# Key pages, key rows and value rows moved in one transfer each, in a hybrid conformer and stick-breaking attention step on one core

## The chip, the core and the metric

The kernel runs on one core of a Trainium2 chip. A core has five engines that run side by side, each through its own instructions in order: TensorE (PE, matmuls into PSUM; PEld is its weight load), VectorE (DVE), ScalarE (ACT), GpSimd (POOL) and SyncE (SP, which here only issues DMA transfers). 16 DMA engines move data between the device's DRAM and SBUF, the on-chip memory of 128 partitions. Engines wait for each other and for transfers by semaphores. The metric is device microseconds of one execution, lower is better.

## The reference

One inference step of a trunk of two layers, for a prompt of 512 new tokens and for 8 sequences that each add 4 tokens to 256 cached ones (their keys and values lie in pages of 128 tokens). Layer 0 mixes tokens by a conformer convolution, layer 1 by stick-breaking attention; each is followed by a gated convolutional FFN. All data is fp32. Cut to the layer that the change touches:

```python
D_MODEL, SEQ, DEC_BATCH, DEC_SEQ, PAST_LEN, PAGE_SIZE, N_HEADS, HEAD_DIM = 1024, 512, 8, 4, 256, 128, 16, 64

def stick_breaking_block(q, k, v, bias, q_start):
    z = einsum('bqhd,bkhd->bhqk', q, k) * HEAD_DIM ** -0.5 + bias[None, :, None, None]
    valid = k_pos[None, :] < q_pos[:, None]
    log_fail = where(valid, log_sigmoid(-z), 0.0)
    after = cumsum(log_fail, axis=3, reverse=True) - log_fail
    weights = where(valid, exp(log_sigmoid(z) + after), 0.0)
    return einsum('bhqk,bkhd->bqhd', weights, v)

# in run_trunk, layer 1
qkv = (h @ attn_w_qkv).reshape(b, t, 3, N_HEADS, HEAD_DIM)
q, k, v = qkv[:, :, 0], qkv[:, :, 1], qkv[:, :, 2]
k_all, v_all = concatenate([k_past, k], 1), concatenate([v_past, v], 1)   # k_past: pages of cache_k by page_table
x = x + stick_breaking_attention(q, k_all, v_all, bias, past_len).reshape(b, t, -1) @ attn_w_o
# k and v of the new tokens are outputs too, as rows (token, head, head_dim)
```

## The kernel before

Activations are kept transposed: `xT`, `qT` and `kT` hold 128 of the 1024 model columns on the partitions, in 8 column blocks `c`, and tokens along the free dimension. A projection takes a block of 256 weight columns of 1 MB (`raw`, loaded by SP, two buffers), splits it on ScalarE and VectorE into a high and a low part (`whi`, `wlo`) and multiplies both by the high and low parts of the activations (`XH`, `XL`), which is the L2163 to L2165 matmuls in the attention layer.

The attention stage works on column blocks `c` (two heads each). For each it projects keys (`keys`) and values (`values`) of the prompt in two halves `h` of 256 and 288 tokens (the second half also has the 32 new tokens of the 8 sequences), then computes logits, scans and products of the pair of heads (`pair`). Beside that the stage works on the cached pages of the 8 sequences:

- `key_page` loads one page of keys, 128 tokens by 1024 numbers, into one of three buffers of `xT`'s memory (`page_t`; the layer's input was saved to DRAM before and is read back at the end, `xsave`). 16 heads lie in four groups of four, `x`; the partition is 32 times the group plus a token number. VectorE then turns blocks of 32 by 32 (L2283), so that the head dimension comes onto the partitions, and a group of matmuls into `dz` (L2301) makes the logits of one pair of sequences from four pages. There are 16 pages and so four dz groups; pages 0 to 2 are asked for before the attention stage, right after `xsave`.
- `keys` copies the projected keys to `kT`, turns them in blocks of 32 by 32 on VectorE (`kr`, two buffers, L2207) and stores them as rows of the output `k_p`, with four transfers for each half (L2212).
- `values` copies the projected values to SBUF on ScalarE (`vT`, L2221), transposes them by two matmuls with the identity (`to_rows`, PSUM tile `one`, L2193) and copies the rows to `vtok` on VectorE (L2225); there they serve the products with the attention weights (`av`, L2494) and are stored to `v_p` (L2228).
- Pages of values are gathered by POOL (L2050) after the pages of keys, into the same three buffers.

The order of the instructions is written by a planner, `Plan`: every operation is entered with its engine, an estimated cost in us and what it reads and writes; `Plan.run` then plays the list through and issues the operations in the order in which they come free, by a priority. The times of `Plan` are estimates only and set the order of instructions on each engine; on the chip each engine follows its own list and waits where it must. For SP, `Plan` counts a fixed 0.7 us until the next issue, and the operation's cost until its data has landed. All of SP's transfers stand in one queue.

Of the kernel before, what the change touches and what calls it, by code (L numbers as in the profile page):

```python
# [9 lines left out]
F32 = mybir.dt.float32  # L10
# [7 lines left out]
P = 128  # L18
# [87 lines left out]
class Plan:  # L106
# [5 lines left out]
    def __init__(self, eager=EAGER, chain=0.0, shifts=""):  # L112
        self.eager = eager
        self.shifts = shifts

        self.chain = chain
        self.ops = []
        self.writes, self.adds, self.reads = {}, {}, {}
        self.rings = {}
        self.follows = {}  # L120
        self.lift, self.urgent = {}, {}
        self.forms, self.change = {}, 0.0
        self.fill = set()

    def op(self, eng, cost, fn, r=(), w=(), a=(), follows=None, lift=0.0, urgent=0.0, after=(), form=None):

        i = len(self.ops)
        deps = set(after)
        for x in r:
            deps |= self.writes.get(x, set()) | self.adds.get(x, set())  # L130
        for x in a:
            if self.reads.get(x):
                self.writes[x] = self.writes.get(x, set()) | self.reads[x] | self.adds.get(x, set())
                self.reads[x], self.adds[x] = set(), set()
            deps |= self.writes.get(x, set())
        for x in w:
            deps |= self.writes.get(x, set()) | self.reads.get(x, set()) | self.adds.get(x, set())
        for x in r:
            self.reads.setdefault(x, set()).add(i)
        for x in a:  # L140
            self.adds.setdefault(x, set()).add(i)
        for x in w:
            self.writes[x], self.reads[x], self.adds[x] = {i}, set(), set()
        for x in (*r, *w, *a):
            b = x[0] if isinstance(x, tuple) else x
            if isinstance(b, Plan.Buf):
                if not b.users and b.before is not None:
                    b.after |= {b.before.users[0]}
                if not b.users and b.old is not None:
                    b.after |= set(b.old.users)  # L150
                deps |= b.after
                b.users.append(i)
        deps.discard(i)
        self.ops.append((eng, cost, fn, deps))
        if lift:
            self.lift[i] = lift
        if urgent:
            self.urgent[i] = urgent
        if follows is not None:
            self.follows[i] = follows  # L160
        if form is not None:
            self.forms[i] = form
        return i

    class Buf:
# [26 lines left out]
    def run(self):  # L192
# [24 lines left out]
        while any(ready.values()):  # L217
# [21 lines left out]
            if eng == "pe":  # L239
                form = self.forms.get(i)  # L240
            last[eng] = i
            free[eng] = t + (cost if eng != "sp" else 0.7)
            for u in users[i]:
                left[u] -= 1
                start[u] = max(start[u], t + cost + self.lag(eng, self.ops[u][0]))
# [5 lines left out]
def tile_trunk(  # L251
# [219 lines left out]
    def uid(s):  # L471
        _n[0] += 1
        return f"{s}_{_n[0]}"
# [1566 lines left out]

    def key_page(t, j):

        pages = cache_k[0, bass.ds(numbers[j], 1)].rearrange("o (q p) (x h) d -> o x p q (h d)", p=32, x=4)
        for x in range(4):
            nc.sync.dma_start(out=t[32 * x:32 * x + 32, :].rearrange("p (q r) -> p q r", q=4), in_=pages[0, x])

    cv = cache_v.rearrange("o n p h d -> (o n p) (h d)")

# [92 lines left out]
    def acost(n):  # L2141
        return 0.1 + n * 0.95e-3
# [41 lines left out]
            prepare(slot + SPLIT_BUFS)  # L2184
        return pt

    def to_rows(src, r):

        rows = psum("one")

        def turn():
            for b in range(2):
                pe.transpose(rows()[:, b * P:(b + 1) * P], src(b), ident)  # L2193

        plan.op("pe", 0.22, turn, r=r, w=[rows])
        return rows, (lambda: rows()[:, :2 * P].rearrange("p (b d) -> p b d", b=2))

    def keys(c, h):
        c0, n = (SA, SB)[h]
        pt = project(k0 + TURNS.index(("k", c)), h)  # L2200
        plan.op("act", acost(256), lambda: act.copy(kT[:, c, c0:c0 + 256], pt()[:, :256]),
                r=[pt], w=[("k", c, h)] + ([("ktp", i) for i in range(4)] if c >= 4 else []))
        if h:
            plan.op("act", 0.2, lambda: act.copy(kT_s[:, c, :], pt()[:, 256:n]), r=[pt], w=[("kT_s", c)])
            plan.op("pool", 1.2, lambda: place_k(c), r=[("kT_s", c)], w=[("kn", c)])
        kr = sbuf("kr", 2 * P, 2)
        plan.op("dve", 0.15 + 256 * 1.1e-3, lambda: dve.transpose(kr(), kT[:, c, c0:c0 + 256]), r=[("k", c, h)], w=[kr])  # L2207

        def store():
            for a in range(4):  # L2210
                rows = slice(32 * a, 32 * a + 32)
                nc.sync.dma_start(out=k_p[0, 0, c0:c0 + 256].rearrange("(b i) h d -> i b (h d)", i=32)[:, :, c * P + 32 * a:c * P + 32 * a + 32],  # L2212
                                  in_=kr()[rows].rearrange("i (b j) -> i b j", j=32))

        plan.op("sp", 7.0, store, r=[kr])

    def values(c, h):
        n = (SA, SB)[h][1]
        pt = project(k0 + TURNS.index(("v", c)), h)
        vt = plan.tile("vT", 2, lambda: vts_.tile([P, SA[1]], F32, tag="vT", name=uid("vT"), bufs=2))  # L2220
        plan.op("act", acost(256), lambda: act.copy(vt(), pt()[:, :256]), r=[pt], w=[vt])  # L2221
        if h:
            plan.op("act", 0.2, lambda: act.copy(vT_s[:, c, :], pt()[:, 256:n]), r=[pt], w=[("vT_s", c)])
        rows, src = to_rows(lambda b: vt()[:, b * P:(b + 1) * P], [vt])
        plan.op("dve", 0.38, lambda: dve.tensor_copy(vtok[c % 3][:, 2 * h:2 * h + 2, :], src()),  # L2225
            r=[rows], w=[("vtok", c % 3, h)])
        if h:
            plan.op("sp", 3.0, lambda: nc.sync.dma_start(out=vpv[:, :, c * P:(c + 1) * P], in_=vtok[c % 3]),  # L2228
                    r=[("vtok", c % 3, 0), ("vtok", c % 3, 1)])

    def new_rows(src, r, dst):

# [12 lines left out]

        plan.op("pe", 0.5, turn, r=r, w=[rows], form="r64")
        plan.op("act", 0.35, lambda: act.copy(new_s, rows()[:, :2 * P]), r=[rows], w=["new", "Qz"])
        plan.op("sp", 3.0, store, r=["new"])


    def page(i):

        t = plan.tile("page", PAGE_BUFS, lambda: page_t[i % PAGE_BUFS])
        if i < PAGE_BUFS:
            plan.op("held", 0.0, lambda: None, w=[t])
            return t
        if i < 2 * NB:
            plan.op("sp", 2.0, lambda: key_page(t(), i), w=[t, ("asked", i)])
        else:
            plan.op("pool", 1.05, lambda: gather(t(), i % (2 * NB), cv), w=[t, ("asked", i)])  # L2260
        plan.op(f"page{i}", 6.0 if i < 2 * NB else 4.0, lambda: None, r=[("asked", i)], w=[(t, 1)])
        return t
# [7 lines left out]
    def page_logits(m):  # L2270
# [17 lines left out]
        def logits():  # L2288
            for odd in range(2):
# [5 lines left out]
                    parts = [(0, KW, kt)]  # L2295
                for e in range(2):
                    for lo, n, src in parts:
                        keys_of = src.rearrange("p (q k j) -> p k q j", k=NC, j=32)
                        for u in range(4):
                            k = 4 * (u % 2) + 2 * (u // 2) + e  # L2300
                            pe.matmul(z()[32 * u:32 * u + 32, (m % 2) * KW + lo:(m % 2) * KW + lo + n],  # L2301
# [322 lines left out]
```

## Time and profile before

| what | value |
|---|---|
| runs | 1256.1, 1256.89, 1257.56 us (median 1256.89) |
| profiled execution | 1256.83 us, of which the span from its first to its last instruction 1255.1 us |
| granted TensorE clock | 0.998 |
| attention stage | from about 585 us (`xsave`) to 831 us (`xT` read back) |
| DMA, whole span | 139661 packets, 142.40 MB, mean 113 GB/s |
| DMA packets under 512 B | 24045 |

The page gives busy times of the engines; a TensorE that is busy all the time is not one at its peak. The share of DMA is the mean over 16 engines. Views of a stretch (from A to B us) give the same sums for that stretch alone: in the DMA row of a stretch each digit is the busy share, in tenths, of a fortieth of it, and the row below it counts packets, and how many of them were under 512 B. In the chain of waits each piece is what the next one waited for.

### The profile page before, as it was taken

The numbers are of one execution on the slowest core, as the hardware profiler recorded it, in microseconds if no ns is written. First come the engines' busy times: TensorE is split into PE (matmuls) and PEld (weight loads), VectorE is DVE, ScalarE is ACT, GpSimd is POOL, SyncE is SP. The second block draws the span as 40 slices with busy tenths as digits, with TensorE's granted clock in tenths as the row PEclk, the third lists the DMA queues.
The fourth block names the chain that finished last, engine by engine and source line by source line (L and its number), as shares of the span: only waits on it lengthen the run. The fifth ranks groups of instructions, "written<-read, shape, count | busy, mean of one in ns | idle before, by whom it ended". The sixth has DMA issues, their size and how long they took to land.

```text
span 1255.1 us, 26652 instructions
## 1 busy us (share of the span) xinstructions
PE 1239.3 (99%) x10742; PEld 1187.2 (95%) x10742; DVE 1011.2 (81%) x1700; ACT 709.8 (57%) x1421; POOL 173.8 (14%) x363
## 2 busy tenths in 40 slices
PE   9999999999999999999999999999999999999997
PEld 8997699999999999999988888999999999999997
DVE  7999887988987886878969897646979987887863
ACT  7793584646655454445545887744636645455453
POOL 5000014111001000000242344000101001000000
PEclk9999999999999999999999999999999999999999
DMA  7455423123233233244379465232123232233121
GB/s 223 129 168 152 129 68 117 35 86 114 80 112 118 68 106 99 92 145 161 97 190 246 128 173 159 71 126 85 49 88 102 93 120 93 80 108 118 60 79 72
DMA packets 139661, 142.40 MB, mean 113 GB/s; under 512 B 24045, under 2 KB 132773, under 8 KB 139266
## 3 DMA queue, kind: packets, MB, share of 16 engines
q1 hardware_dynamic: 133134, 120.29, 32.1%
q0 software_dynamic: 6400, 20.41, 5.2%
q8 instruction: 84, 1.38, 0.5%
q14 instruction: 39, 0.32, 0.1%
q10 hardware_dynamic: 4, 0.01, 0.0%
HBM read 129.34 MB, written 12.18 MB: 113 GB/s over the span
## 4 chain that ended last, share of the span: by engine, by line
PE 81%; DVE 14%; DMA 2%; ACT 2%; issue 1%; SPq 0%; POOL 0%; DVEq 0%; ACTq 0%
PE acc L1635 5%; PE acc L1634 5%; PE acc L1633 5%; PE acc L759 4%; PE acc L760 4%; PE acc L761 4%; PE av L896 3%; DVE wlo L401 3%; PE av L1412 3%; PE av L1413 3%; PE av L1414 3%; PE tr L1413 3%; PE tr L1412 3%; PE tr L1414 3%; PE tr L1633 3%; PE tr L1635 3%
## 5 line engine op out<-in xcount | busy, mean ns | idle before, releaser
L398 ACT CAST whi<-raw 128x1024 fp32r<-128x1024 f32 (+2 forms) x247 | 224.7, 913 | 123.5 <-PE av L1413 24.8
L401 DVE TENSOR_TENSOR wlo<-raw,whi 128x1024 fp32r<-128x1024 f32 (+2 forms) x247 | 258.7, 1050 | 33.0 <-ACT whi L398 31.5
L759 PE MATMUL acc<-XH,whi 128*128 128x288 f32 (+1 forms) x384 | 112.7, 294 | 0.0
L761 PE MATMUL acc<-XH,wlo 128*128 128x288 f32 (+1 forms) x384 | 110.3, 287 | 0.9 <-DVE wlo L401 0.9
L760 PE MATMUL acc<-XL,whi 128*128 128x288 f32 (+1 forms) x384 | 110.3, 287 | 0.0
L1412 PE MATMUL av<-HH,whi 128*128 128x288 f32 (+1 forms) x280 | 83.2, 297 | 0.5 <-DVE xT L1735 0.5
L1413 PE MATMUL av<-HL,whi 128*128 128x288 f32 (+1 forms) x280 | 82.6, 295 | 0.0
L1635 PE MATMUL acc<-TH,wlo 128*128 128x272 f32 x288 | 82.6, 287 | 0.0
L1634 PE MATMUL acc<-TL,whi 128*128 128x272 f32 x288 | 82.6, 287 | 0.0
L1633 PE MATMUL acc<-TH,whi 128*128 128x272 f32 x288 | 82.5, 287 | 0.0
L1414 PE MATMUL av<-HH,wlo 128*128 128x288 f32 (+1 forms) x280 | 82.2, 293 | 0.0
L1682 ACT COPY G<-acc 128x272 f32<-128x272 f32 (+1 forms) x72 | 26.8, 372 | 93.8 <-PE acc L1635 93.8
L2163 PE MATMUL acc<-XH,whi 128*128 128x256 f32 (+1 forms) x264 | 79.7, 302 | 0.0
L1412 PE MATMUL tr<-HH,whi 128*128 128x256 f32 (+1 forms) x280 | 78.5, 280 | 0.0
L1413 PE MATMUL tr<-HL,whi 128*128 128x256 f32 (+1 forms) x280 | 78.4, 280 | 0.0
L1414 PE MATMUL tr<-HH,wlo 128*128 128x256 f32 (+1 forms) x280 | 78.3, 280 | 0.0
L2165 PE MATMUL acc<-XH,wlo 128*128 128x256 f32 (+1 forms) x264 | 75.7, 287 | 0.0
L2164 PE MATMUL acc<-XL,whi 128*128 128x256 f32 (+1 forms) x264 | 75.7, 287 | 0.0
L759 PEld LDWEIGHTS acc<-XH,whi 128*128 128x128 f32 x384 | 72.2, 188 | 1.4 <-issue 0.4
L761 PEld LDWEIGHTS acc<-XH,wlo 128*128 128x128 f32 x384 | 72.1, 188 | 1.1 <-DVE wlo L401 1.1
L760 PEld LDWEIGHTS acc<-XL,whi 128*128 128x128 f32 x384 | 72.2, 188 | 0.3
L1573 DVE SCALAR_TENSOR_TENSOR cv<-G,fprm,cv 128x560 f32<-128x560 f32 x88 | 69.5, 797 | 0.5
(464 smaller groups left out, 4343.0 us busy)
## 6 DMA issues: line engine op xcount, KB each, us to landing
raw<-in_ffn_w_gate_dram SPq DMA_DIRECT2D x22, 1024.0 KB
raw<-in_ffn_w_up_dram SPq DMA_DIRECT2D x22, 1024.0 KB
raw<-in_ffn_w_down_dram SPq DMA_DIRECT2D x24, 768.0 KB
raw<-in_attn_w_qkv_dram SPq DMA_DIRECT2D x12, 1024.0 KB
xT<-in_cache_k_dram SPq DMA_DIRECT2D x64, 128.0 KB
raw<-in_conv_w_in_dram POOLq DMA_DIRECT2D x6, 1024.0 KB, 6.8
rep<-glu SPq DMA_DIRECT2D x36, 142.0 KB
raw<-in_conv_w_out_dram POOLq DMA_DIRECT2D x4, 1024.0 KB, 6.4
```

The costliest lines, as they stand in the source:

```text
L398: act.copy(hi[:, k, :], src[:, k])
L401: dve.tensor_tensor(lo[:, k, :], src[:, k], hi[:, k, :], op=ALU.subtract)
L759: pe.matmul(o, hi[:, k, :], XH[:, k, c0:c0 + n], start=(k == 0), stop=False)
L760: pe.matmul(o, hi[:, k, :], XL[:, k, c0:c0 + n], start=False, stop=False)
L761: pe.matmul(o, lo[:, k, :], XH[:, k, c0:c0 + n], start=False, stop=(k == NC - 1))
L1412: pe.matmul(o, hi[:, j + k, :], xh, start=(start and k == 0), stop=False, **kw)
L1413: pe.matmul(o, hi[:, j + k, :], xl, start=False, stop=False, **kw)
L1414: pe.matmul(o, lo[:, j + k, :], xh, start=False, stop=(stop and k == len(xs) - 1), **kw)
L1633: pe.matmul(o, hi[:, j + k, :], xh, start=(start and k == 0), stop=False, **kw)
L1634: pe.matmul(o, hi[:, j + k, :], xl, start=False, stop=False, **kw)
L1635: pe.matmul(o, lo[:, j + k, :], xh, start=False, stop=(k == 3), **kw)
L2163: pe.matmul(o, hi[:, k, :], XH[:, k, c0:c0 + n], start=(k == 0), stop=False)
```

## The change

Three things are rewritten, and the costs that `Plan` is given with them.

- A key page is one transfer instead of four. The partition is still 32 times the group of heads plus a token number, but now four consecutive tokens lie on a partition (token 4p + q at partition p of its group, part q) where it was every 32nd (token 32q + p). The dz matmuls therefore read the transposed page with the token part q innermost, at a step of 256 numbers.
- Key rows are one transfer for each half instead of four. VectorE's transposition takes every eighth token into a block of 32, so that partition 32a + i of `kr` holds tokens 8i to 8i + 7 of head part a, and the target is written as part, token, number: 4 x 256 x 32.
- Value rows no longer go through TensorE. VectorE transposes blocks straight from PSUM (`vT`, now the transposed blocks), one transfer for each half stores them to a scratch of 512 x 128 in DRAM (`vrows`, three buffers), and one transfer for each `c` reads the scratch back as `vtok`. The copy on ScalarE, the two matmuls and the copy on VectorE go.
- `hold` lets an operation of SP count more than 0.7 us until the next issue (1.9 for the rows of new tokens).

```diff
-            free[eng] = t + (cost if eng != "sp" else 0.7)
+            free[eng] = t + (cost if eng != "sp" else self.hold[i])
...
     def key_page(t, j):
-        pages = cache_k[0, bass.ds(numbers[j], 1)].rearrange("o (q p) (x h) d -> o x p q (h d)", p=32, x=4)
-        for x in range(4):
-            nc.sync.dma_start(out=t[32 * x:32 * x + 32, :].rearrange("p (q r) -> p q r", q=4), in_=pages[0, x])
+        nc.sync.dma_start(out=t, in_=cache_k[0, bass.ds(numbers[j], 1)].rearrange("o t (x h) d -> (o x) t (h d)", x=4))
...
     def keys(c, h):
...
-        plan.op("dve", 0.15 + 256 * 1.1e-3, lambda: dve.transpose(kr(), kT[:, c, c0:c0 + 256]), r=[("k", c, h)], w=[kr])
+        plan.op("dve", 0.15 + 256 * 1.1e-3, lambda: dve.transpose(kr().rearrange("p (b i) -> p b i", i=32), kT[:, c, c0:c0 + 256].rearrange("p (i b) -> p b i", i=32)), r=[("k", c, h)], w=[kr])
         def store():
-            for a in range(4):
-                rows = slice(32 * a, 32 * a + 32)
-                nc.sync.dma_start(out=k_p[0, 0, c0:c0 + 256].rearrange("(b i) h d -> i b (h d)", i=32)[:, :, c * P + 32 * a:c * P + 32 * a + 32],
-                                  in_=kr()[rows].rearrange("i (b j) -> i b j", j=32))
-        plan.op("sp", 7.0, store, r=[kr])
+            nc.sync.dma_start(out=k_p[0, 0, c0:c0 + 256].rearrange("t h d -> t (h d)")[:, c * P:(c + 1) * P].rearrange("t (a j) -> a t j", a=4),
+                              in_=kr())
+        plan.op("sp", 5.0, store, r=[kr])
     def values(c, h):
         pt = project(k0 + TURNS.index(("v", c)), h)
-        vt = plan.tile("vT", 2, lambda: vts_.tile([P, SA[1]], F32, tag="vT", name=uid("vT"), bufs=2))
-        plan.op("act", acost(256), lambda: act.copy(vt(), pt()[:, :256]), r=[pt], w=[vt])
-        rows, src = to_rows(lambda b: vt()[:, b * P:(b + 1) * P], [vt])
-        plan.op("dve", 0.38, lambda: dve.tensor_copy(vtok[c % 3][:, 2 * h:2 * h + 2, :], src()),
-            r=[rows], w=[("vtok", c % 3, h)])
+        vb = plan.tile("vT", 2, lambda: vts_.tile([P, 256], F32, tag="vT", name=uid("vT"), bufs=2))
+        plan.op("dve", 0.15 + 256 * 1.1e-3, lambda: dve.transpose(
+            vb().rearrange("p (b i) -> p b i", i=32), pt()[:, :256].rearrange("p (i b) -> p b i", i=32)), r=[pt], w=[vb])
+        if not h:
+            vrows[c] = plan.tile("vrows", 3, lambda: scratch.tile([SEQ, P], F32, tag="vrows", name=uid("vrows"), bufs=3))
+        d = vrows[c]
+        plan.op("sp", 5.0, lambda: nc.sync.dma_start(out=d()[c0:c0 + 256].rearrange("t (a j) -> a t j", a=4), in_=vb()), r=[vb], a=[d])
+        if not h:
+            return
+        plan.op("sp", 5.0, lambda: nc.sync.dma_start(out=vtok[c % 3], in_=d().rearrange("(b p) d -> p b d", p=P)),
+                r=[d], w=[("vtok", c % 3, 0), ("vtok", c % 3, 1)])
         plan.op("sp", 3.0, lambda: nc.sync.dma_start(out=vpv[:, :, c * P:(c + 1) * P], in_=vtok[c % 3]),
...
-        plan.op("sp", 3.0, store, r=["new"])
+        plan.op("sp", 4.0, store, r=["new"], hold=1.9)
...
-            plan.op("sp", 2.0, lambda: key_page(t(), i), w=[t, ("asked", i)])
+            plan.op("sp", 0.7, lambda: key_page(t(), i), w=[t, ("asked", i)])
...
-                        keys_of = src.rearrange("p (q k j) -> p k q j", k=NC, j=32)
+                        keys_of = src.rearrange("p (g q k j) -> p k g j q", q=4, k=NC, j=32)
```

The costs change the planner's order. SP's list around pages 3 to 8, before (`ISA` computes a page's address, `xT` is the page's buffer, `raw` a block of weights; sizes are those of the target):

```order
L2045 ISA
L2045 DMA xT<-in_cache_k_dram 32x4x256
L2212 DMA out_dram<-kr_8353 32x8x32 x4
L361 DMA raw_8377<-in_attn_w_qkv_dram 128x8x256
L2212 DMA out_dram<-kr_8364 32x8x32 x4
```

and now, from page 5 on:

```order
L2045 DMA xT<-in_cache_k_dram 128x4x256
L2201 DMA out_dram<-kr_8338 4x256x32
L363 DMA raw_8360<-in_attn_w_qkv_dram 128x8x256
L2201 DMA out_dram<-kr_8350 4x256x32
L2045 ISA
L2045 DMA xT<-in_cache_k_dram 128x4x256
L2201 DMA out_dram<-kr_8408 4x256x32
L2201 DMA out_dram<-kr_8461 4x256x32
```

Page 5 is now asked for ahead of the first key rows, and pages 6 to 8 stand behind or among them; each page and each store is one row instead of four.

SP's list now around page 9, where the first value rows go out and come back:

```order
L2215 DMA vrows_8517<-vT_8507 4x256x32
L2045 ISA
L2045 DMA xT<-in_cache_k_dram 128x4x256
L2215 DMA vrows_8517<-vT_8544 4x256x32
L2219 DMA vtok_8229<-vrows_8517 128x4x128
L2045 ISA
L2045 DMA xT<-in_cache_k_dram 128x4x256
L2201 DMA out_dram<-kr_8649 4x256x32
L2221 DMA out_dram<-vtok_8229 128x4x128
```

Page 10 stands behind the read back of the scratch (L2219), which waits for the two stores to it (L2215).

TensorE's list after the first dz group, before:

```order
L2301 MATMUL dz_8477<-e_8421,xT 32x128 x4
L2193 MATMUL one_8514<-ident,vT_8505 128x128 x2
L2432 MATMUL z_8518<-kT,qT 128x384
L2432 MATMUL z_8520<-kT,qT 128x384
L2432 MATMUL z_8518<-kT,qT 128x128
L2432 MATMUL z_8520<-kT,qT 128x128
L2163 MATMUL acc_8524<-XH,whi_8159 128x288
```

and now:

```order
L2294 MATMUL dz_8436<-e_8391,xT 32x128 x4
L2425 MATMUL z_8468<-kT,qT 128x384
L2425 MATMUL z_8470<-kT,qT 128x384
L2425 MATMUL z_8468<-kT,qT 128x128
L2425 MATMUL z_8470<-kT,qT 128x128
L2163 MATMUL acc_8412<-XH,whi_8150 128x256
```

The two transposing matmuls are gone and the dz group stays where it was; from the first dz group to the fourth both orders have the same 222 projection matmuls.

More of the change, by code (lines that the diff above doesn't have):

```diff
@@ L123, in __init__, with op @@
         self.fill = set()
-    def op(self, eng, cost, fn, r=(), w=(), a=(), follows=None, lift=0.0, urgent=0.0, after=(), form=None):
+        self.hold = {}
+    def op(self, eng, cost, fn, r=(), w=(), a=(), follows=None, lift=0.0, urgent=0.0, after=(), form=None, hold=0.7):
         i = len(self.ops)
@@ L162, in op @@
             self.forms[i] = form
+        self.hold[i] = hold
         return i
@@ L2185, in project @@
         return pt
[L2187 to L2196, printed above, removed]
+    vrows = {}
     def keys(c, h):
@@ L2215, in keys @@
-        plan.op("sp", 7.0, store, r=[kr])
+            nc.sync.dma_start(out=k_p[0, 0, c0:c0 + 256].rearrange("t h d -> t (h d)")[:, c * P:(c + 1) * P].rearrange("t (a j) -> a t j", a=4),
+                              in_=kr())
+        plan.op("sp", 5.0, store, r=[kr])
     def values(c, h):
-        n = (SA, SB)[h][1]
+        c0, n = (SA, SB)[h]
         pt = project(k0 + TURNS.index(("v", c)), h)
-        vt = plan.tile("vT", 2, lambda: vts_.tile([P, SA[1]], F32, tag="vT", name=uid("vT"), bufs=2))
@@ L2221, in values @@
-        plan.op("act", acost(256), lambda: act.copy(vt(), pt()[:, :256]), r=[pt], w=[vt])
-        if h:
-            plan.op("act", 0.2, lambda: act.copy(vT_s[:, c, :], pt()[:, 256:n]), r=[pt], w=[("vT_s", c)])
-        rows, src = to_rows(lambda b: vt()[:, b * P:(b + 1) * P], [vt])
-        plan.op("dve", 0.38, lambda: dve.tensor_copy(vtok[c % 3][:, 2 * h:2 * h + 2, :], src()),
-            r=[rows], w=[("vtok", c % 3, h)])
-        if h:
-            plan.op("sp", 3.0, lambda: nc.sync.dma_start(out=vpv[:, :, c * P:(c + 1) * P], in_=vtok[c % 3]),
-                    r=[("vtok", c % 3, 0), ("vtok", c % 3, 1)])
+        vb = plan.tile("vT", 2, lambda: vts_.tile([P, 256], F32, tag="vT", name=uid("vT"), bufs=2))
@@ L2231, in new_rows @@
+        plan.op("act", 0.2, lambda: act.copy(vT_s[:, c, :], pt()[:, 256:n]), r=[pt], w=[("vT_s", c)])
+        plan.op("sp", 5.0, lambda: nc.sync.dma_start(out=vtok[c % 3], in_=d().rearrange("(b p) d -> p b d", p=P)),
+                r=[d], w=[("vtok", c % 3, 0), ("vtok", c % 3, 1)])
+        plan.op("sp", 3.0, lambda: nc.sync.dma_start(out=vpv[:, :, c * P:(c + 1) * P], in_=vtok[c % 3]),
+                r=[("vtok", c % 3, 0), ("vtok", c % 3, 1)])
     def new_rows(src, r, dst):
```

## The prediction

> **What bounds the kernel now.** I read the page first, then the stretches by stage, the chain of waits, and last the DMA view of short stretches in which only one kind of transfer runs.
>
> ```profile
> span 1255.1 us, 26652 instructions
> ...
> PE 1239.3 (99%) x10742; PEld 1187.2 (95%) x10742; DVE 1011.2 (81%) x1700; ACT 709.8 (57%) x1421; POOL 173.8 (14%) x363
> ```
>
> TensorE is busy 99% of the span, so a saving elsewhere is worth nothing unless TensorE waits for it. But a share of the whole span hides one stage. The attention stage, cut in two at the last key page:
>
> ```profile
> 637.00:693.00 56.00, 53.15 (x530) 47.11 (x529) 45.17 (x55) 27.67 (x50) 19.27 (x63) 1.00 0.95 232
> 697.00:823.00 126.00, 125.64 (x1297) 107.56 (x1290) 102.29 (x152) 99.53 (x177) 39.94 (x55) 1.00 0.44 129
> ```
>
> The columns are length, busy time of PE, PEld, DVE, ACT and POOL, granted clock, DMA share, GB/s. In the first stretch the 16 DMA engines are 95% busy and TensorE is idle for 56.00 - 53.15 = 2.85 us; in the second DMA is at 44% and TensorE never waits. So the first stretch already stands at the edge of being DMA-bound, and the chain says by what:
>
> ```profile
> 640.11 5.27 DMA xT<-in_cache_k_dram
> ...
> 647.20 4.65 DMA out_dram<-kr
> ...
> 673.19 0.22 PE one L2193 x2
> ...
> 696.08 1.87 PE dz L2301 x48
> ```
>
> Two of its long pieces are the two transfers that the change rewrites: a key page (5.27 us) and key rows (4.65 us). The stretch begins with the issue of pages 3 and 4 (page 0 to 2 are there before) and ends when page 15 has landed and VectorE transposes it:
>
> ```profile
> 637.14 4.73 SPq L2045 DMA_DIRECT2D xT<-in_cache_k_dram  x8
> ...
> L2283 DVE STREAM_TRANSPOSE e<-xT x8: 1204/1232/1247, 638.2 to 692.1; 128x1024 f32<-128x1024 f32 x8
> ```
>
> So 13 pages come in from 637.1 to 692.1, 55 us. Each engine runs in order, and the fourth dz group (696.08) needs page 15: whatever moves that page moves everything after it.
>
> **How many DMA engines one transfer uses.** This decides the case, so I look at it in stretches with few transfers. First three stores of 30 rows x 2 pieces (60 pieces of 512 B), then four stores whose target starts with a dimension of 8 (64 pieces of 512 B), then the 12 loads of the first three key pages (32 partitions x 4 pieces of 1 KB each), three weight loads (128 x 8 pieces of 1 KB), and a stretch with eight of today's key-row stores (256 pieces of 128 B each):
>
> ```profile
> DMA packets 225, 0.09 MB, mean 13 GB/s; under 512 B 45, under 2 KB 225, under 8 KB 225
> ...
> DMA  0002552000000045400000002552000000155300
> DMA packets 288, 0.13 MB, mean 47 GB/s; under 512 B 32, under 2 KB 288, under 8 KB 288
> q1 hardware_dynamic: 288, 0.13, 16.3%
> ...
> DMA  0006888794789998999998931000000000000000
> GB/s 0 0 0 138 246 260 176 243 340 132 231 225 310 211 240 176 211 222 246 208 219 190 231 70 26 9 15 15 0 0 0 0 0 0 0 0 0 0 0 0
> DMA packets 1731, 1.61 MB, mean 115 GB/s; under 512 B 192, under 2 KB 1728, under 8 KB 1728
> q1 hardware_dynamic: 1728, 1.57, 48.3%
> ...
> DMA  0008999970000000000479999003699990000000
> GB/s 0 0 0 111 297 362 389 384 232 0 0 0 0 0 0 0 14 0 0 92 207 375 386 386 295 7 0 60 212 364 387 384 357 12 0 0 0 0 0 0
> DMA packets 3123, 3.19 MB, mean 133 GB/s; under 512 B 48, under 2 KB 3120, under 8 KB 3120
> q1 hardware_dynamic: 3120, 3.15, 40.5%
> ...
> q1 hardware_dynamic: 2176, 0.26, 24.4%
> ```
>
> Beside its data every transfer has a few tiny packets: 45/3 = 15 for the stores of 60 pieces, 32/4 = 8 for those that start with 8, 192/12 = 48/3 = 16 for the loads over 32 or 128 partitions. The stores with 8 also never pass 5 tenths of the 16 engines, where the loads reach 9. I read this as one closing packet per engine used, and the count as the largest number up to 16 that divides the outermost sizes of both sides: 8 and 32 give 8, 60 and 30 give 15, 32 and 32 give 16. After the change a key page reads a source that starts with 4 (the four groups of heads) into 128 partitions; key rows and value rows are written to targets that start with 4 from 128 partitions. By these rows all three run on 4 engines instead of 16. The Trainium skill's "DMA: Bandwidth & Descriptors" says the same in "Rules for kernel authors": an outermost dimension under 16 confines the whole DMA to that many engines.
>
> Prices, as time of one engine per piece: page 0.483 x 14 x 16 / 1536 = 70 ns, weight 0.405 x 24 x 16 / 3072 = 51 ns, key row 0.244 x 7 x 16 / 2048 = 13.3 ns, 512 B piece 0.163 x 2.8 x 16 / 256 = 28 ns (stretches of 14, 24, 7 and 2.8 us).
>
> **The change part by part.**
>
> Key pages: 64 loads become 16, each with 512/4 = 128 pieces on each of four engines: 128 x 70 ns = 9.0 us instead of 512/16 x 70 ns = 2.25 us. The price could also be that of a weight piece, 51 ns (6.5 us). I take 70 ns, the page's own: the loads over 32 partitions run at some 220 GB/s where those over 128 reach 385, and the four engines go through four such quarters side by side. The Trainium skill's "SBUF — State Buffer" ("Door 1: The DMA port swizzle") lets partitions 0 to 31 and 32 to 63 share ports; by it engines in step meet at a port and 70 ns stays, without it 51 ns and 1338 us, as below.
>
> Key rows: 64 stores become 16, each 1024/4 = 256 pieces per engine, 256 x 13.3 ns = 3.4 us instead of 0.85. Value rows: 16 such stores to the scratch are new, 3.4 us each; 8 reads back (512 pieces of 512 B over 16 engines, 32 x 28 ns = 0.9 us) are new; each must wait on SP until its two stores have landed, and what stands behind it on SP (pages, weights) waits too. The trace has no such wait; stores of this size from POOL land after
>
> ```profile
> out_dram<-row POOLq DMA_DIRECT2D x6, 48.0 KB, 2.4
> ```
>
> so I take 2.4 us; it is 0 at best and 4.65 us at worst (the chain's key rows).
>
> All of these and the weights stand in one queue. Between page 3 and page 15 the changed SP order holds 13 pages, 5 key-row stores, 4 value-row stores, 3 weight loads, 2 reads back and 1 store of them. On each of the four engines: 13 x 9.0 + 9 x 3.4 + 3 x 3.2 + 3 x 0.9 + 2 x 2.4 + 2.4 for the last landing = 117.0 + 30.6 + 9.6 + 2.7 + 4.8 + 2.4 = 167 us. Only three page buffers exist, but the queue is never empty, since page n needs page n-3 transposed and that lands two pages earlier. Page 15 lands at 637.1 + 167 = 804 instead of 692: +112 us, none of it covered, because TensorE's work between the first and the fourth dz group is the same 222 projection matmuls in both orders.
>
> Value transposes: 16 pairs at 0.22 us leave TensorE. Five pairs stand ahead of the fourth dz group and now fall into its wait; 11 x 0.22 = -2.4 us. The copies around them:
>
> ```profile
> L2207 DVE STREAM_TRANSPOSE kr<-kT 128x256 f32<-128x256 f32 x16 | 6.8, 431 | 6.4 <-DMA out_dram<-kr 3.2 <-ACT vT L2221 2.3 <-ACT kT L2201 1.0
> L2225 DVE COPY vtok<-one 128x256 f32<-128x256 f32 x16 | 6.6, 411 | 2.1 <-PE one L2193 1.9
> L2221 ACT COPY vT<-acc 128x256 f32<-128x256 f32 x16 | 6.0, 374 | 7.7 <-PE acc L2165 7.4
> ```
>
> ScalarE loses 16 x 374 ns, VectorE swaps 16 copies (411 ns) for 16 block transposes (431 ns). Transposes now read every eighth element; no row shows what that costs. Between nothing and double, 32 x 0.43 = 13.8 us, two thirds of it in the second stretch, where VectorE is idle for 126 - 102 = 24 us: nothing on the path.
>
> Page logits read the keys with a step of 1 KB. A dz group takes 1.87 us now; between unchanged and four times, I take double. The first three groups stand in the page wait, the last adds 1.9 us (0 to 5.6).
>
> SP issues 0.59 us per page load (4.73/8); 72 fewer issues free SP, which waits for the queue anyway: nothing.
>
> Second stretch: the last read back comes after the last projection, +2.4 us.
>
> Sum, from the profiled execution of 1256.83 us (span 1255.1; the median of the runs is 1256.89): 1256.8 + 112 - 2.4 + 1.9 + 2.4 = **1371 us**.
>
> **The rivals.**
>
> A: the page piece costs 51 ns on four engines. For it: only four engines write, and half of them may drift apart. Against: the page's own rows. 13 x 6.5 = 84.5 instead of 117.0, page 15 at 771.5, 1338 us. At the best rate of the weight loads (389 GB/s over 16 engines, 42 ns) it is 5.4 us a page, 70 us, 1324 us: the low end.
>
> B: the second stretch becomes queue-bound too. It holds 23 of the 3.4 us stores (78), 5 weight loads (16), 12 reads back and their stores (11), and the value gathers of POOL on every engine:
>
> ```profile
> q0 software_dynamic: 2132, 7.75, 19.2%
> ```
>
> 0.192 x 126 = 24 us; in all 129 us in 126, and six waits of 2.4 us beside them: +17 us, 1388 us. Against: the last stores have no reader, so some 14 us of them may come late.
>
> C, the other side: the transfers are not confined, or different transfers take different engines. Then a page over 128 partitions runs at the weight's price, 512/16 x 51 ns = 1.6 instead of 2.25 us; 13 x 0.65 = 8.5 us less queue against 4 x 0.85 + 2 x 2.4 us of new work in the first stretch: its 2.85 us of idle TensorE go and 16 x 0.22 = 3.5 us of transposes, 1250.5 us. It decides from the point where a page takes under some 4 us. The Trainium skill's "DMA: Bandwidth & Descriptors" ("Rules for kernel authors") also speaks for it: many small transfers should be coalesced, and one transfer over 128 partitions is better than several over parts. Against it: 15, 8 and 16 tiny packets per transfer, without exception in these stretches.
>
> **How the numbers follow.** A difference of 0.2% (2.5 us) is about what a measurement here can tell from none. My forecast 0.48, A 0.25, B 0.15, C 0.07, later than B 0.05. Low end 1322 (the best page rate of A), high end 1392 (B and its unknown wait). Faster comes from C alone, 0.05; same 0.02, if C's new waits eat its gain; slower 0.93.
>
> **What would show it.** Right: about three times as long between the issue of page 3 and the transposition of page 15, with VectorE waiting for the page loads and TensorE idle for most of 110 us there; a DMA share near 0.25 to 0.35 in that stretch; 4 tiny packets per page. Wrong: page loads that land within 4 us of the one before (C), or TensorE waiting on dz matmuls that have their pages, or a wait that sits in the second stretch on av products for vtok (B).

## The result, and the profile after

The changed kernel takes 1349.04 us (median of 6 runs, 1346.35 to 1355.01) against 1257.32 us of the kernel before: 1.0733 times as long, 95% interval 1.071 to 1.0757. The profiled execution took 1350.21 us. Forecast were 1371 us, in a range of 1322 to 1392.

The page after, its head first, then the shares of the chain of waits:

```profile
span 1348.5 us, 26383 instructions
PE 1261.1 (94%) x10710; PEld 1201.3 (89%) x10710; DVE 1014.6 (75%) x1700; ACT 704.5 (52%) x1405; POOL 171.3 (13%) x363
...
PE 69%; DVE 15%; DMA 12%; ACT 2%; issue 2%; POOL 0%; SPq 0%; DVEq 0%; ACTq 0%
```

TensorE is busy 22 us longer (1261.1 against 1239.3), although it has 32 instructions fewer, and idle 72 us longer. The two stretches of the attention stage, cut again where page 15 is there and where the reload of `xsave` begins (columns as in the prediction):

```profile
637.00:772.00 135.00, 75.12 (x563) 62.91 (x561) 48.18 (x56) 28.02 (x48) 20.36 (x72) 0.78 0.39 107
772.00:916.00 144.00, 129.90 (x1277) 110.07 (x1278) 105.78 (x156) 98.12 (x169) 40.17 (x56) 0.94 0.53 133
```

In the first, TensorE is idle 59.88 us where it was idle 2.85; in the second 14.1 us where it was idle 0.36. The granted clock was 0.78 and 0.94 where it was 1.00, and the projection matmuls of L2165 took 317 ns in the first stretch where they took 287. The chain of waits in the first stretch and behind it, after, and then the end of the second stretch before:

```profile
638.32 10.92 DMA xT<-in_cache_k_dram
649.24 13.46 DMA out_dram<-kr
662.70 13.48 DMA xT<-in_cache_k_dram
677.46 10.88 DMA xT<-in_cache_k_dram
695.19 11.80 DMA vrows<-vT
...
708.05 8.58 DMA xT<-in_cache_k_dram
...
720.45 19.67 DMA xT<-in_cache_k_dram
741.40 13.55 DMA xT<-in_cache_k_dram
...
758.63 12.36 DMA xT<-in_cache_k_dram
772.31 1.90 PE dz L2294 x23
...
809.19 13.94 DMA out_dram<-kr
...
915.81 8.74 DMA xT<-xsave
```

```profile
822.94 8.19 DMA xT<-xsave
```

The nine transfers shown from 638.32 on sum to 114.7 of the 134 us up to the fourth dz group: pages, key rows and value rows in one queue, and no TensorE work stands in the chain between them. What TensorE waited for in this stretch, after and then before:

```profile
PE t L2467 <- DVE e L2460: 22.0, 4, 16.5
PE acc L2163 <- DVE vT L2210: 20.7, 2, 16.3
PE z L2425 <- ACT e L2431: 9.2, 1, 9.2
PE dz L2294 <- DVE e L2276: 8.3, 4, 3.3
```

```profile
PE t L2474 <- DVE e L2467: 1.4, 1, 1.4
PE one L2193 <- ACT vT_s L2223: 1.4, 1, 1.4
```

(Each row gives us in total, the number of waits and the longest.) The dz groups themselves wait for only 8.3 of the 60 us. Most of the rest is attention weights (`t` for `e`) and accumulators that VectorE has yet to empty (`acc` for `vT`). VectorE works in order, and in this stretch it waits for pages and for `kr` to be stored:

```profile
DVE e L2276 <- DMA xT<-in_cache_k_dram: 55.2, 7, 13.7
DVE kr L2198 <- DMA out_dram<-kr: 18.1, 2, 13.2
```

The fourth dz group starts at 772.31 instead of 696.08 (+76.2). The `xsave` reload comes 143.5 us later instead of 126.9 (+16.6). After it the two kernels take 434.4 and 433.9 us. 76.2 + 16.6 + 0.5 = 93.3 us, against 1350.21 - 1256.83 = 93.4: the whole loss lies in these two stretches, 82% of it ahead of the fourth dz group.

VectorE's transpositions of the pages, with the wait for the loads, and the DMA view of the first page loads of the changed kernel:

```profile
L2276 DVE STREAM_TRANSPOSE e<-xT x8: 1201/1245/1246, 639.3 to 771.0; 128x1024 f32<-128x1024 f32 x8
...
  DMA xT<-in_cache_k_dram: 68.4, 10
```

```profile
DMA  0001322222224222222232222222222222222222
GB/s 0 0 0 35 86 57 78 74 90 82 90 92 125 90 90 88 76 92 70 82 84 74 70 84 74 82 84 88 86 90 90 92 92 90 92 92 92 90 92 92
DMA packets 1506, 1.56 MB, mean 78 GB/s; under 512 B 8, under 2 KB 1503, under 8 KB 1503
...
q1 hardware_dynamic: 1503, 1.53, 24.6%
```

Only pages move in this stretch of 20 us. The DMA row stands at 2 tenths (a quarter of 16 engines) where it stood at 6 to 9, and two finished pages left 8 tiny packets, 4 each: four engines, as the prediction read from the packet counts. Its price was off: 0.246 x 20 x 16 = 78.7 us for 1495 pieces, 52.6 ns each and not 70. A page takes 128 x 52.6 ns = 6.7 us, not 9.0. By the 90 GB/s of the later slices it is less, 45.5 ns for each piece and 5.8 us for a page.

### The profile page after: what moved, and what is told of

Its sections match the earlier page's. It is cut to its first block, busy times and chain, and to the rows that moved or that the text cites. A ratio compares the mean times of both kernels' runs of the same rounds, so it can differ in the third digit from the quotient of the medians.

```text
span 1348.5 us, 26383 instructions
## 1 busy us (share of the span) xinstructions
PE 1261.1 (94%) x10710; PEld 1201.3 (89%) x10710; DVE 1014.6 (75%) x1700; ACT 704.5 (52%) x1405; POOL 171.3 (13%) x363
## 4 chain that ended last, share of the span: by engine, by line
PE 69%; DVE 15%; DMA 12%; ACT 2%; issue 2%; POOL 0%; SPq 0%; DVEq 0%; ACTq 0%
DMA xT<-in_cache_k_dram 7%; PE acc L1637 5%; PE acc L1636 5%; PE acc L1635 5%; PE acc L761 3%; PE acc L762 3%; PE acc L763 3%; DVE wlo L403 3%; PE av L898 3%; PE av L1414 3%; PE av L1415 3%; PE av L1416 3%; PE tr L1415 2%; PE tr L1414 2%; PE tr L1416 2%; PE tr L1635 2%
## 5 line engine op out<-in xcount | busy, mean ns | idle before, releaser
L2163 PE MATMUL acc<-XH,whi 128*128 128x256 f32 (+1 forms) x264 | 84.2, 319 | 20.8 <-DVE vT L2210 20.7
L2164 PE MATMUL acc<-XL,whi 128*128 128x256 f32 (+1 forms) x264 | 79.3, 301 | 0.0
L2165 PE MATMUL acc<-XH,wlo 128*128 128x256 f32 (+1 forms) x264 | 79.3, 300 | 0.0
L2163 PEld LDWEIGHTS acc<-XH,whi 128*128 128x128 f32 x264 | 53.6, 203 | 26.4 <-DVE vT L2210 21.3
L761 PEld LDWEIGHTS acc<-XH,whi 128*128 128x128 f32 x384 | 72.2, 188 | 1.4 <-issue 0.4
```

Of the source, the lines that this page charges most:

```text
L761: pe.matmul(o, hi[:, k, :], XH[:, k, c0:c0 + n], start=(k == 0), stop=False)
L2163: pe.matmul(o, hi[:, k, :], XH[:, k, c0:c0 + n], start=(k == 0), stop=False)
```

## The experiments

Twelve kernels in three groups. "Page 15" is the start of its transposition by VectorE: 692.1 us in the kernel before, 771.0 after.

**Group 1: engines given back, one kind of transfer at a time.**

`pages_16`: the changed kernel, each page load cut in four of 32 partitions (token order kept).

```diff
-        nc.sync.dma_start(out=t, in_=cache_k[0, bass.ds(numbers[j], 1)].rearrange("o t (x h) d -> (o x) t (h d)", x=4))
+        pages = cache_k[0, bass.ds(numbers[j], 1)].rearrange("o (p q) (x h) d -> o x p q (h d)", q=4, x=4)
+        for x in range(4):
+            nc.sync.dma_start(out=t[32 * x:32 * x + 32, :].rearrange("p (q r) -> p q r", q=4), in_=pages[0, x])
```

> The changed kernel with each key page split again into four transfers, one for each group of heads (32 partitions on both sides), in the new token order; stores, scratch and the order of the instructions as changed. Theory (four DMA engines for a transfer with an outermost 4, all in one queue): a page costs the queue 2.25 us instead of 6, page 15 is transposed near 716 instead of 771, the second stretch stays at some 143 us, in all about 1295 us. Rival (the waits for the read back on SP, the stepped reads and the new order cost the time, whatever the number of engines): within 10 us of 1350.

Measured: 1295.25 us (ratio 1.0298, 1.028 to 1.0317), page 15 at 718.6. The same bytes to the same places, and 54 us less. Page 15 comes 52.4 us earlier, 4.0 us for each of 13 pages.

`stores_16`: the changed kernel, key-row and value-row stores cut in four, by 32 partitions each.

```diff
-            nc.sync.dma_start(out=k_p[0, 0, c0:c0 + 256].rearrange("t h d -> t (h d)")[:, c * P:(c + 1) * P].rearrange("t (a j) -> a t j", a=4),
-                              in_=kr())
+            for a in range(4):
+                nc.sync.dma_start(out=k_p[0, 0, c0:c0 + 256].rearrange("(i b) h d -> i b (h d)", b=8)[:, :, c * P + 32 * a:c * P + 32 * a + 32],
+                                  in_=kr()[32 * a:32 * a + 32].rearrange("i (b j) -> i b j", j=32))
...
(the value-row store in the same way)
```

> The changed kernel with the key-row and value-row stores split into four transfers of 32 partitions each, pages in one transfer as changed. Theory: nine stores ahead of page 15 cost 0.85 instead of 3.4 us, page 15 near 742, and the second stretch goes back to about 127 us since no store holds up VectorE; about 1306 us. Rival (waits, steps and order): within 10 us of 1350.

Measured: 1315.33 us (1.0458, 1.0439 to 1.0477), page 15 at 747.6. 34 us less, 9 us short of what was expected; the second stretch (748 to 879) is 131 us long, against 144 in the changed kernel.

`all_16`: both cuts together.

> Both splits: pages, key rows and value rows in four transfers of 32 partitions each; the value rows still go by VectorE and the DRAM scratch, the dz matmuls still read with a step of 1 KB, and the order of the instructions is the changed one. Theory: page 15 near 694, second stretch near 127 us, 1250 to 1260 us. Rival (waits, steps and order): at least 1330 us.

Measured: 1285.3 us (1.0218, 1.0204 to 1.0232), page 15 at 717.2. This expectation missed: with all 16 engines 28 us of loss are left. Four engines explain 1349 - 1285 = 64 of the 92 us, not all of them. The two savings overlap: 54 and 34 us alone, 64 together. Groups 2 and 3 look for the rest.

**Group 2: one part of the change put into the kernel before.**

`page_alone`: the single page transfer, with the token order and the stepped dz read that it needs.

```diff
-        pages = cache_k[0, bass.ds(numbers[j], 1)].rearrange("o (q p) (x h) d -> o x p q (h d)", p=32, x=4)
-        for x in range(4):
-            nc.sync.dma_start(out=t[32 * x:32 * x + 32, :].rearrange("p (q r) -> p q r", q=4), in_=pages[0, x])
+        nc.sync.dma_start(out=t, in_=cache_k[0, bass.ds(numbers[j], 1)].rearrange("o t (x h) d -> (o x) t (h d)", x=4))
...
-                        keys_of = src.rearrange("p (q k j) -> p k q j", k=NC, j=32)
+                        keys_of = src.rearrange("p (g q k j) -> p k g j q", q=4, k=NC, j=32)
```

> The kernel before with one part of the change: a key page in one transfer (and the dz matmuls with the step of 1 KB that goes with it). Theory: 13 pages of 6 us and 7 key-row stores of 0.85 us, page 15 near 735, about 1300 us. Rival (what costs is the stepped dz read, not the page): 1260 to 1265 us.

Measured: 1302.94 us (1.036, 1.0341 to 1.0379), page 15 at 740.7: +45 us. Its two stretches:

```profile
637.00:741.00 104.00, 72.51 (x571) 62.44 (x573) 45.94 (x56) 30.34 (x56) 21.58 (x72) 0.85 0.47 130
741.00:869.00 128.00, 127.64 (x1305) 109.02 (x1298) 103.95 (x155) 99.51 (x177) 41.05 (x56) 1.00 0.43 124
```

The loss is ahead of page 15; the second stretch is 128 us against 126.

`step_alone`: only the token order and the stepped dz read; the page still comes in four loads over 16 engines.

```diff
-        pages = cache_k[0, bass.ds(numbers[j], 1)].rearrange("o (q p) (x h) d -> o x p q (h d)", p=32, x=4)
+        pages = cache_k[0, bass.ds(numbers[j], 1)].rearrange("o (p q) (x h) d -> o x p q (h d)", q=4, x=4)
...
-                        keys_of = src.rearrange("p (q k j) -> p k q j", k=NC, j=32)
+                        keys_of = src.rearrange("p (g q k j) -> p k g j q", q=4, k=NC, j=32)
```

> The kernel before with only the token order of the key pages changed: four consecutive tokens on a partition, still four loads of 32 partitions, and the dz matmuls read with a step of 1 KB; both orders of instructions are otherwise the same. Theory (a stepped read doubles a dz group, 3.9 instead of 1.87 us, and TensorE pays it): 4 x 2 us, 1262 to 1266 us. Rival (three of the four groups stand in the 2.85 us of idle time or before a page that lands later): 1257 to 1260 us.

Measured: 1266.37 us (1.0066, 1.0052 to 1.0079), page 15 at 703.2: +8.8 us with the instructions in the order of before. The dz matmuls by line, of the kernel before and of `step_alone` (min/median/max in ns):

```profile
L2301 PE MATMUL dz<-e,xT x128: 272/273/273, 647.8 to 697.7; 128*32 128x128 f32 x128
L2301 PE MATMUL dz<-kT,xT x64: 379/379/403, 646.9 to 696.7; 128*32 128x256 f32 x64
```

```profile
L2301 PE MATMUL dz<-e,xT x128: 396/397/420, 649.9 to 707.8; 128*32 128x128 f32 x128
L2301 PE MATMUL dz<-kT,xT x64: 613/656/786, 648.1 to 705.8; 128*32 128x256 f32 x64
```

and one dz group in the chain of each, before and in `step_alone`:

```profile
696.08 1.87 PE dz L2301 x48
```

```profile
704.36 3.87 PE dz L2301 x46
```

Reading the keys at a step of 1 KB takes TensorE 1.45 to 1.73 times as long per matmul and doubles a group. Four groups at +2.0 us make 8 us. TensorE is idle for 3.5 us ahead of page 15 (637 to 703), hardly more than the 2.85 before, so it pays in busy time: where pages do not wait on four engines nothing hides the first three groups.

`keyrows_alone`: the single key-row store, with the stepped transposition.

```diff
-        plan.op("dve", 0.15 + 256 * 1.1e-3, lambda: dve.transpose(kr(), kT[:, c, c0:c0 + 256]), r=[("k", c, h)], w=[kr])
+        plan.op("dve", 0.15 + 256 * 1.1e-3, lambda: dve.transpose(kr().rearrange("p (b i) -> p b i", i=32), kT[:, c, c0:c0 + 256].rearrange("p (i b) -> p b i", i=32)), r=[("k", c, h)], w=[kr])
...
+            nc.sync.dma_start(out=k_p[0, 0, c0:c0 + 256].rearrange("t h d -> t (h d)")[:, c * P:(c + 1) * P].rearrange("t (a j) -> a t j", a=4),
+                              in_=kr())
```

> The kernel before with one part of the change: key rows in one transfer on four engines (and the transposition of every eighth token). Theory: seven stores of the page stretch cost the queue 3.4 instead of 0.85 us, 18 us in a stretch whose engines are 95% busy, and TensorE pays most of it, 1268 to 1277 us. Rival (the four engines have room, since the pages use all 16): within 3 us of 1257.

Measured: 1264.7 us (1.0056, 1.0038 to 1.0074), page 15 at 701.8: +7.1, less than expected. The 18 us of the expectation counted seven stores. By the rows of SP five are issued ahead of page 15's loads and two behind them; five at 2.55 us more each, not covered, would have cost 13. Page 15 comes 9.7 us later.

`keyrows_step`: the stepped transposition without the single store (the four stores of before, to rows 8 apart).

> The kernel before with the stepped key-row transposition alone (VectorE reads every eighth element), stores still over 16 engines with 32 partitions each. Theory 1 (VectorE has room): 650 instead of 431 ns for 16 transposes, nothing on the path, 1256 to 1259 us. Theory 2 (VectorE's extra 0.22 us falls on the path ahead of page 15, seven of them, or the stores' targets 16 KB apart land later): 1259 to 1262 us. With 1 the +7.1 us of keyrows_alone is all the four engines'.

Measured: 1260.41 us (1.0024, 1.0014 to 1.0035), page 15 at 696.5. VectorE's group in it:

```profile
L2207 DVE STREAM_TRANSPOSE kr<-kT 128x256 f32<-128x256 f32 x16 | 10.4, 658 | 7.1 <-DMA out_dram<-kr 6.2 <-ACT kT L2201 0.9
```

658 ns instead of 431, and VectorE waits longer for its stores to free `kr` (6.2 us, before 3.2); +3.1 us together, so the step with its other target rows is not hidden. The run does not part these two. By difference some 4 of `keyrows_alone`'s 7.1 us are then the four engines'.

`values_alone`: the value rows by VectorE and the scratch, their stores cut in four over 16 engines (pages and key rows as before).

```diff
+        vb = plan.tile("vT", 2, lambda: vts_.tile([P, 256], F32, tag="vT", name=uid("vT"), bufs=2))
+        plan.op("dve", 0.15 + 256 * 1.1e-3, lambda: dve.transpose(
+            vb().rearrange("p (b i) -> p b i", i=32), pt()[:, :256].rearrange("p (i b) -> p b i", i=32)), r=[pt], w=[vb])
...
+            for a in range(4):
+                nc.sync.dma_start(out=d()[c0:c0 + 256].rearrange("(i b) k -> i b k", b=8)[:, :, 32 * a:32 * a + 32],
+                                  in_=vb()[32 * a:32 * a + 32].rearrange("i (b j) -> i b j", j=32))
```

> The kernel before with one part of the change: value rows by VectorE, scratch and read back, the stores to the scratch in four transfers of 32 partitions; key pages and key rows as before. Theory (a saving on TensorE, paid by SP, which issues 64 stores and 8 reads more at about 0.6 us each and waits eight times for stores to land): 3.5 us less on TensorE against some 5 to 15 us of later pages, 1258 to 1270 us. Rival (the value path is a gain once its stores are spread, and what is left over in the kernel with all transfers spread comes from the steps): 1253 to 1256 us.

Measured: 1265.8 us (1.0063, 1.0048 to 1.0078), page 15 at 708.2. Its stretches:

```profile
637.00:708.00 71.00, 58.82 (x534) 52.08 (x533) 45.60 (x56) 26.49 (x46) 22.33 (x71) 0.89 0.82 201
708.00:830.00 122.00, 121.90 (x1257) 104.40 (x1257) 102.07 (x150) 98.07 (x168) 44.35 (x56) 1.00 0.59 158
```

The second stretch is shorter than before (122 against 126 us, TensorE busy 121.90), but not all of that is the gain of the value transposes: the stretch holds 40 matmuls fewer, of which 22 are value transposes and the others are work that now lies elsewhere. From 637 to the reload of `xsave` TensorE is busy 181.2 us instead of 182.7, so the gain is some 1.6 us. Page 15 is 16 us later, with TensorE idle for 12 us ahead of it, and the part loses 8.

`page_128`: the kernel before with a page as 128 token rows of 4 KB in one transfer over 16 engines. It leaves out bringing the heads to their partitions, so the logits of the cached pages are not the right ones; all instructions run.

```diff
+        nc.sync.dma_start(out=t.rearrange("p (x r) -> p x r", x=4), in_=cache_k[0, bass.ds(numbers[j], 1)].rearrange("o t (x h) d -> (o t) x (h d)", x=4))
```

> The kernel before with each key page loaded in one transfer of 128 partitions from 128 token rows, which uses 16 engines (the heads are not brought to their partitions, so the logits of the cached pages are left out as a result; all instructions run). Theory (a page piece costs 70 ns only because 16 engines write into 32 partitions): pieces near 46 to 51 ns, the page stretch no longer at the edge, up to 2.8 us of TensorE's idle time gone, 1254 to 1257 us. Rival (70 ns is the price of reading the cache): 70 ns again, 1257 us.

Measured: 1254.27 us (0.9973, 0.9963 to 0.9984). The DMA view of its first page loads:

```profile
DMA packets 451, 1.61 MB, mean 115 GB/s; under 512 B 64, under 2 KB 64, under 8 KB 448
...
q1 hardware_dynamic: 448, 1.57, 31.8%
```

Of the 64 tiny packets 16 end at 592.0 to 592.2, before the first piece of a page moves; 48 are left for 3 pages, 16 each: 16 engines. 0.318 x 14 x 16 / 1536 = 46 ns for each KB, where the loads of before take 70. One transfer per page is no loss when it has 16 engines; its gain, 3.3 us, is about the size of TensorE's idle time ahead of page 15 (2.85 us before, 0.2 here). Pieces are 4 KB here and go to 128 partitions, so it does not say which of the two makes them cheaper.

**Group 3: do the parts add, and what is left at 16 engines?**

`pages_keyrows`: the kernel before with `page_alone` and `keyrows_alone` together.

> The kernel before, with key pages and key rows in one transfer each (four engines, stepped reads), and the value rows left as before. Theory 1 (each transfer has its own price, the sum holds): page_alone's +45.4 and keyrows_alone's +7.1 add to 1257 + 52.5 = 1310 us, page 15 transposed at 740.7 + 9.7 = 750. Theory 2 (one queue on four engines is the bound, so each of the 9 key-row stores ahead of page 15 now costs its full 2.55 us more instead of hiding): 740.7 + 23 = 764 and 1326 us. By either, what is left up to 1349 us is the value rows' part: 39 or 23 us.

Measured: 1316.96 us (1.0475, 1.0459 to 1.0491). Its last page:

```profile
L2279 DVE STREAM_TRANSPOSE e<-xT x8: 1208/1246/1399, 638.6 to 752.0; 128x1024 f32<-128x1024 f32 x8
```

Theory 2 had counted nine key-row stores; by the rows of SP five are issued ahead of page 15's loads here too. With five its figures are 740.7 + 12.8 = 753.5 for page 15 and 1257 + 45.4 + 12.8 = 1315 us. Page 15 at 752.0 lies between this and the sum (750), and the time, +59.6, is nearer to it than to the +52.5 of theory 1: beside pages on four engines the key-row stores cost about their full price.

`values_spread`: the changed kernel with the value-row stores alone cut in four over 16 engines.

> The changed kernel with the value-row stores alone cut into four of 32 partitions (16 engines); key pages and key rows stay on four engines. Theory 1 (the value-row stores lengthen the one queue while they are on four engines): 16 x 2.55 us = 41 us of queue go, some 10 to 13 us of them ahead of page 15, which is transposed at about 758 to 761, and the total falls to 1318 to 1330 us. Theory 2 (what costs is the wait on the sync queue for the scratch stores to land, not their engines): more issues, same waits, 1342 to 1352 us.

Measured: 1325.91 us (1.055, 1.0534 to 1.0566), page 15 at 756.4. Theory 1: four engines under the value-row stores alone cost 1349 - 1326 = 23 us. So the loss builds up as 1257 + 59.6 (pages and key rows) + 9.0 (value path over 16 engines, with the new order on SP) + 23.1 (its stores on four) = 1349. These are differences from one kernel to the next, so the sum closes by itself; another order of the steps would give other shares.

`all_16_pool`: `all_16` with the value-row stores issued by GpSimd; TensorE, VectorE and ScalarE keep their order.

```diff
-                nc.sync.dma_start(out=d()[c0:c0 + 256].rearrange("(i b) k -> i b k", b=8)[:, :, 32 * a:32 * a + 32],
+                nc.gpsimd.dma_start(out=d()[c0:c0 + 256].rearrange("(i b) k -> i b k", b=8)[:, :, 32 * a:32 * a + 32],
```

> The kernel of all_16 (pages, key rows and value rows all on 16 engines) with the 64 value-row stores issued by GpSimd instead of the sync queue; the order on TensorE, VectorE and ScalarE is the same. Theory 1 (what is left of the loss there, 28 us, is the sync queue's issue time, some 0.62 us for each transfer, some 16 to 20 of them ahead of page 15): page 15 is transposed at about 706 instead of 717 and the time falls from 1285 to 1270 to 1276 us. Theory 2 (the rest is the stepped reads of TensorE and VectorE and the round trip through the scratch): 1283 to 1288 us, page 15 still at about 717.

Measured: 1280.29 us (1.0188, 1.0174 to 1.0202; runs from 1277.08 to 1282.84). Its last page, then that of `all_16`:

```profile
L2285 DVE STREAM_TRANSPOSE e<-xT x8: 1203/1242/1247, 638.4 to 707.3; 128x1024 f32<-128x1024 f32 x8
```

```profile
L2285 DVE STREAM_TRANSPOSE e<-xT x8: 1201/1245/1247, 639.8 to 717.2; 128x1024 f32<-128x1024 f32 x8
```

Page 15 comes 10 us earlier, as theory 1 said, but the median is only 5 us lower and 1270 to 1276 was not reached. The two figures do not belong together: the profiled execution is the fastest of its five (1277.08) and that of `all_16` the slowest of its five (1287.86), and these two are 10.8 us apart. So the issue time of the sync queue is worth some 5 us, and the traces show no place where more was lost. At 16 engines, if the parts add, the 28 us are: dz step 8.8, key-row step with its target rows 3.1, value path 8.2, issue time of the sync queue 5 (part of which may lie in the 8.2); 3 us or more have no experiment, and neither has the new order of the instructions by itself.

## Why the prediction was right, and where its terms were off

The cause was the forecast one: outermost sizes of 4 put all three transfers on four engines, the queue set page 15, and TensorE waited there. Packet counts of 4 per page, a DMA row at 2 tenths, VectorE 68.4 us behind page loads, and 64 us coming back with 16 engines all show it. The path was wider than forecast: not the dz groups alone but all that VectorE hands to TensorE stood behind the pages. Three signs came smaller or larger than named: page 3 to page 15 took 2.4 times as long and not three times, TensorE was idle for 60 us and not for most of 110, and the DMA share was 0.39 where 0.25 to 0.35 was forecast. Rival C is out: the waits for pages in the chain are 8.6 to 19.7 us long, where it spoke of landings within 4. By its terms:

- **Price of a page piece (70 ns): too high by a third.** It was 52.6 ns, rival A's. 13 x 128 x 17.4 ns = 29 of the 33 us by which page 15 came earlier than forecast (771 against 804). A's 771.5 was met to half a microsecond. By the 45.5 ns of the later slices it would be 41 us, so the other terms would have been 8 us short; `pages_16` points the same way, with 4.0 us a page more than over 16 engines, where 32 x 54 ns = 1.7 us are left, 5.7 together. The term that was mis-sized is the choice between the two rows: the 70 ns had been read while twelve loads ran at once on 16 engines at some 220 GB/s; alone on four, the piece costs what a weight piece costs. The Trainium skill's "SBUF — State Buffer" ("Door 1: The DMA port swizzle") has partitions 0 to 31 and 32 to 63 share ports. That engines in step would meet there was the prediction's inference, and the trace does not bear it out: four engines move 90 GB/s together, 22.5 each, nearly the sixteenth of the weight loads' 385 GB/s (24) and well over that of the 220 GB/s (14) which 70 ns stood for.

- **The queue is never empty: not quite.** SP waited for the scratch stores longer than the 2.4 us taken from GpSimd's stores. They stand behind pages in the queue: these waits are 12.1 us here, 5.7 with the stores alone over 16 engines (`stores_16`) and 2.2 with the pages too (`all_16`). SP's waits from 637 to 772 and its rows around one of them:

```profile
SPq L2219 <- DMA vrows<-vT: 12.1, 3, 9.9
```

```profile
695.19 1.53 SPq L2215 DMA_DIRECT2D vrows<-vT  x1
707.08 0.37 SPq L2219 DMA_DIRECT2D vtok<-vrows  x1
708.05 0.61 SPq L2045 DMA_DIRECT2D xT<-in_cache_k_dram  x1
```

 In the chain this wait stands with 11.80 us (695.19), and the next page is issued only after it. The forecast charged 2 x 2.4 for it. That the total of page 15 still fell on A's number is therefore partly chance: at 52.6 ns a piece some other term must have been too long, at 45.5 ns the waits that were too short make up the difference.

- **Stepped dz read (+1.9, range 0 to 5.6): the factor was right, its place only here.** A group went from 1.87 to 3.87 us. In the changed kernel the page wait hides three of four groups, as said; alone it costs 8.8 us.

- **Stepped VectorE transpositions (nothing): not confirmed.** 658 ns instead of 431, within the bound of double, but together with their stores' new target rows not hidden: +3.1 us in `keyrows_step`. The cover that the prediction named lay in the second stretch; the cost showed ahead of page 15 (696.5 instead of 692.1). Which of the two costs it stays open.

- **Value transposes (-2.4): about right in size.** TensorE is busy 1.6 us less in `values_alone`. The later pages ahead of it eat the gain.

- **Second stretch (+2.4): too low; rival B was right in size (+17, measured +16.6), not in place.** B's sum counted all stores of the stretch, but its sign was a wait on the value side. TensorE's waits after page 15 (770 to 930), then VectorE's, and one of them in VectorE's order:

```profile
PE t L2467 <- DVE e L2460: 10.7, 1, 10.7
PE av L2487 <- DMA vtok<-vrows: 1.5, 1, 1.5
```

```profile
DVE kr L2198 <- DMA out_dram<-kr: 14.9, 3, 9.1
```

```profile
819.02 0.64 DVE L2198 STREAM_TRANSPOSE kr<-kT 128x256 f32<-128x256 f32 x1 [9.10 <-DMA out_dram<-kr]
```

 The sign that the prediction gave for B, av products waiting for vtok, is there with 1.5 us only. The long wait goes another way: key-row stores on four engines hold the two `kr` buffers (the 13.94 us at 809.19 in the chain), VectorE stands in order behind them, and the attention weights that TensorE needs (`t` for `e`) stand behind VectorE. The prediction said that the last stores have no reader; but their buffers have a next writer. The waits for `kr` and TensorE's waits for `t` in the second stretch fall together in the other traces: 14.9 and 10.7 us here, 9.9 and 6.8 in `pages_16`, 7.6 and 4.2 in `values_spread`, 3.5 and 1.7 in `stores_16`, where the stretch is 131 us long. With key rows on four engines and no value-row stores (`pages_keyrows`) it is 128 us, so key rows alone do not do it. That 17 and 16.6 agree is partly chance: of the 16.6 us some 3 are TensorE busy longer (129.8 against 126.5 us, at a clock of 0.94), which B did not count.

Put together against 1371: -33 at page 15 (of it 29 the page's price), +12.2 behind it (579.2 from page 15 to the end of the profiled execution, where the forecast had 1371 - 804 = 567), 1350. The two errors had opposite signs, and the hit owes something to that.

## What to carry to other kernels

Before several transfers become one, look at the outermost size of both sides after the rearrangement, and count the closing packets of a transfer in the trace: 4 means four engines, whatever the bytes. A layout that makes the transfer simple moves its step into the engines that read it, and that has a price for each instruction (TensorE 1.45 to 1.73 times, VectorE 1.5 times from SBUF here) which wants a row of its own. A store without a reader is still waited for where its buffer is used again on an engine that runs in order.

## What the hardware showed that was not expected

- The same page piece of 1 KB costs 70 ns with twelve loads of 32 partitions at once on 16 engines and 52.6 ns on four engines. With the token order of `pages_16`, still 32 partitions and 16 engines, it is 0.371 x 14 x 16 / 1536 = 54 ns, with the engines at 3 to 7 tenths:

```profile
q1 hardware_dynamic: 1729, 1.57, 37.1%
```

 So the 70 ns are not the price of 32 partitions as such. Whether it is how many pieces are in flight at a time or the order of the rows in memory stays open.

- VectorE's block transposition pays for a step in SBUF (431 to 658 ns), but with the same step read from an accumulator in PSUM it takes 446 ns, hardly more than from SBUF without a step (no run has PSUM without a step). Here in `values_spread`:

```profile
L2210 DVE STREAM_TRANSPOSE vT<-acc 128x256 f32<-128x256 f32 x16 | 7.1, 446 | 3.8 <-PE acc L2165 3.3 <-ACT vT_s L2224 0.4
```
